# Half-width score products, a written TensorE order and a ScalarE copy in a gated-linear-attention stage

## The chip, the cores and the metric

The kernel runs on one core of a Trainium2 chip. The metric is the device time of one execution in microseconds (us), the median over several runs. A core has TensorE (matrix products; PE in the profile, with PEld for its weight loads), VectorE (DVE), ScalarE (ACT), GpSimd (POOL) and SyncE (SP), which issues most of the DMA transfers. Operands lie in SBUF tiles; TensorE's results go to PSUM, which this kernel uses as eight banks of 128 partitions by 512 float32 values. Each engine has its own list of instructions, and semaphores order one engine's behind another's.

## What is computed

The reference is a two-layer decoder trunk over 512 tokens of width 1024, in float32. Layer 0 mixes by windowed attention and a short convolution, layer 1 by gated linear attention (GLA); each layer has a gated feed-forward block with a convolution and a gated embedding. The change lies wholly in GLA, which has 4 heads with keys of 128 and values of 256:

```
log_a = log_sigmoid(g_lr @ w_gate_up + gate_bias) / 16
def step(state, inp):                    # one chunk of tokens, one head
    g = cumsum(log_a)
    o_inter = (q * exp(g)) @ state
    scores[t, s] = sum_d q[t, d] * k[s, d] * exp(g[t, d] - g[s, d])   for s <= t
    o_intra = scores @ v
    state = exp(g_end) * state + (k * exp(g_end - g)).T @ v
o = rms_norm(o_inter + o_intra) * silu(og);  y = o @ w_out
```

## The kernel before, in words

Activations lie feature by token: a tile holds 128 features by 512 tokens. A projection is `mm3` (L153): both operands are split into a high and a low part, and three products (L157 to L159) add up in one PSUM bank. Weights come through `weights`, `raw` and `cut` (L109 to L151): SyncE loads up to 1 MB into one of two `raw` buffers, ScalarE writes the high parts (`wh`, L137) and VectorE the low parts (`wl`, L138), with three buffers each. PSUM is used as four banks `ps` for projections and four banks `pa` for everything else.

`mixer1` (L1075) is the GLA stage. `query`, `key` and `gate` (L1121 to L1135) are projections of 24 products of 128x512 each, `Values` (L1086) makes the values in two steps of 48 products. For the scores the tokens are taken in NT = 4 blocks of 128. Within a block the pairs s < t are covered by levels b = 64, 32, ..., 1: level b holds the pairs in which s lies in the first and t in the second half of the same 2b tokens. For each head h:

- `base` (L1201): the running sum G of the log decays (VectorE, L1204), then the product of keys and queries of the even tokens (L1211), summed over features on TensorE with a matrix of ones (L1213) and written by VectorE to the diagonal of `sc` (L1215), which GpSimd has zeroed (L1214).
- `decay` (L1221), levels 64 to 4: a tile F whose first halves are k exp(G_mid - G) and whose second halves are q exp(G - G_mid); VectorE and ScalarE take turns.
- `level` (L1238): products of F with itself. For b < 64 one product per block, with all 128 columns of the block as weights and the 64 columns of the second halves moving (L1246); VectorE copies only the wanted entries to `sc` under a mask (L1253). For b = 64 a product of 64 weight columns by 64 (L1249), copied by L1255.
- `decay_pairs` and `level_pairs` (L1257, L1274): levels 2 and 1 share one product of 128x128 per block (L1280). For it VectorE scales every other key in place, and GpSimd copies the scaled queries into every other query (L1272). Two masked copies follow (L1284, L1289).
- `decay_off`, `off` (L1295, L1319): factors to and from the block borders, three transposes on TensorE (L1324) and a copy by ScalarE (L1326).
- `state` (L1329): three products (L1337). Products 0 and 1 go to the two halves of one `pa` bank, product 2 to another; ScalarE copies product 0 out (L1344), VectorE adds the other two to the state (L1339).
- `read` (L1349): for each block j the scores times the values (L1360), plus the state's part for j > 0 (L1362). Blocks 0 and 1 share a bank, and so do 2 and 3. ScalarE sums the squares of each (L1364, an activation and a read of its accumulator), the root goes through GpSimd (L167), and VectorE scales (L1369).
- `turn` and `gated` (L1371, L1137): eight transposes (L1376) which ScalarE copies out (L1380), then the product with silu(og) (L1142) and its split.

The calls stand in a list at the end of `mixer1`. Tile, the layer that records the kernel, chooses each engine's order from priorities and its own estimates, so that instructions may leave the order of the list; it places the semaphore waits, and it lets an access to a PSUM bank wait for the access to the same bank that was recorded before it. Inside `tc.manual_schedule(engines={...})` the engines named keep the recorded order; `setup`, the attention stage and the last stage use that already.

A float32 product that isn't a transpose runs as two passes, each with its own weight load, so its count in the profile is twice that of the code.

Of the kernel before, what the change touches and what calls it, by code (L numbers as in the profile page):

```python
# [18 lines left out]
P = 128  # L19
S = 512  # L20
# [36 lines left out]
class Kernel:  # L57
# [1017 lines left out]
    def mixer1(self):  # L1075
# [4 lines left out]
        with tc.tile_pool(name="m1", bufs=1) as mp:  # L1080
# [31 lines left out]
            def pair_w(c0):  # L1112
                return self.weights(w_in[:, :, c0 : c0 + 256], ND, 256)
# [82 lines left out]

            first = lambda x, b: x.rearrange("p (n b) -> p n b", b=2 * b)[:, :, :b]
            second = lambda x, b: x.rearrange("p (n b) -> p n b", b=2 * b)[:, :, b:]
            scores, Gs, Fs = {}, {}, {}

            def base(h):  # L1201

                G = Gs[h] = mp.tile([P, S], F32, tag="G", name=self.nm("G"), bufs=2)
                nc.vector.tensor_tensor_scan(  # L1204
                    G, run.rearrange("p a b -> p (a b)"), las[h], 0.0, op0=ALU.mult, op1=ALU.add
                )
                sc = scores[h] = mp.tile([P, GDV * NT], F32, tag="sc", name=self.nm("sc"), bufs=3)

                pr = new()[:, : S // 2]
                ev = lambda x: x.rearrange("p (n b) -> p n b", b=2)[:, :, 0]  # L1210
                nc.vector.tensor_tensor(pr, ev(kT[h]), ev(qT[h]), ALU.mult)  # L1211
                pd = self.pa()[:, : S // 2]
# [25 lines left out]
            def level(h, levels):  # L1238
                A = scores[h][:, :S]
                for l in levels:  # L1240
                    b, F = LEVELS[l], Fs[h, l]
                    pl = self.pa()
                    for t in range(NT):
                        c = slice(t * P, (t + 1) * P)
                        if b < 64:
                            mm(second(pl[:, c], b), F[:, c], second(F[:, c], b), start=True, stop=True)  # L1246
                        else:
                            mid = t * P + b
                            mm(pl[:b, mid : mid + b], F[:, t * P : mid], F[:, mid : mid + b], start=True, stop=True)  # L1249
                    if b < 64:  # L1250
                        mk = second(msk[:, l, :], b).unsqueeze(1).to_broadcast([P, NT, 64 // b, b])
                        tv = lambda x: x.rearrange("p (t n b) -> p t n b", t=NT, b=2 * b)[:, :, :, b:]
                        nc.vector.copy_predicated(tv(A), mk, tv(pl))  # L1253
                    else:
                        nc.vector.tensor_copy(second(A[:b], b), second(pl[:b], b))  # L1255

            def decay_pairs(h):  # L1257


                G, k, q = Gs[h].rearrange("p (n b) -> p n b", b=4), kT[h], qT[h].rearrange("p (n b) -> p n b", b=4)  # L1260
                G2 = Gs[h].rearrange("p (n b) -> p n b", b=2)
                E = new()
                Ek, Eq = E[:, : S // 2], E[:, S // 2 :].rearrange("p (n b) -> p n b", b=2)
                nc.vector.tensor_tensor(Ek, G2[:, :, 1], G2[:, :, 0], ALU.subtract)
                nc.vector.tensor_tensor(
                    Eq, G[:, :, 2:], G[:, :, 1:2].to_broadcast([P, S // 4, 2]), ALU.subtract
                )
# [3 lines left out]
                nc.vector.tensor_tensor(Eq, Eq, q[:, :, 2:], ALU.mult)  # L1271
                nc.gpsimd.tensor_copy(q.rearrange("p n (u b) -> p n u b", b=2)[:, :, :, 0], Eq)  # L1272

            def level_pairs(h):  # L1274

                A = scores[h][:, :S]
                pl = self.pa()
                for t in range(NT):
                    c = slice(t * P, (t + 1) * P)
                    mm(pl[:, c], kT[h][:, c], qT[h][:, c], start=True, stop=True)  # L1280
                v4 = lambda x: x.rearrange("p (t n b) -> p t n b", t=NT, b=4)
                m4 = lambda l: msk[:, l, :].rearrange("p (n b) -> p n b", b=4)
                two, one = LEVELS.index(2), LEVELS.index(1)
                nc.vector.copy_predicated(  # L1284
                    v4(A)[:, :, :, 2:], m4(two)[:, :, 2:].unsqueeze(1).to_broadcast([P, NT, P // 4, 2]),
                    v4(pl).rearrange("p t n (u b) -> p t n u b", b=2)[:, :, :, :, 0],
                )
                v2 = lambda x: x.rearrange("p (t n b) -> p t n b", t=NT, b=2)[:, :, :, 1]
                nc.vector.copy_predicated(  # L1289
                    v2(A),  # L1290
                    msk[:, one, :].rearrange("p (n b) -> p n b", b=2)[:, :, 1].unsqueeze(1).to_broadcast([P, NT, P // 2]),
                    v2(pl),
                )

            def decay_off(h):  # L1295
                G, b = Gs[h], 64
# [22 lines left out]
            def off(h):  # L1319

                Es, Ec, tot = Fs[h, "off"]
                pt = self.pa()
                for i in range(NT - 1):
                    nc.tensor.transpose(pt[:, i * P : (i + 1) * P], Es[:, i * P : (i + 1) * P], self.ident)  # L1324
                kt = new()
                nc.scalar.copy(kt[:, : 3 * P], pt[:, : 3 * P])  # L1326
                Fs[h, "kt"] = kt
# [74 lines left out]
            key(w, 0)  # L1402
            key(w, 1)
            w = pair_w(256)
            base(0)
            decay(0, lo)
            query(w, 2)
            level(0, lo)
            decay(0, hi)
            decay_off(0)  # L1410
            decay_pairs(0)
            query(w, 3)
            w = pair_w(768)
            level(0, hi)
            level_pairs(0)
            off(0)
            base(1)
            decay(1, lo)
            key(w, 2)
            level(1, lo)  # L1420
            decay(1, hi)
            decay_off(1)
            decay_pairs(1)
            key(w, 3)
            v = Values(0, 336, 336)
            level(1, hi)
            level_pairs(1)
            off(1)
            v.step(0)
            base(2)  # L1430
            decay(2, lo)
            v.step(1)
            v = Values(336, 672, 336)
            state(0)
            level(2, lo)
            read(0)
            decay(2, hi)
            decay_off(2)
            decay_pairs(2)
            v.step(0)  # L1440
            level(2, hi)
            level_pairs(2)
            off(2)
            turn(0)
            base(3)
            decay(3, lo)
            v.step(1)
            w = pair_w(2064)
            state(1)
            level(3, lo)  # L1450
            read(1)
            decay(3, hi)
            decay_off(3)
            decay_pairs(3)
            gate(w, 0)
            level(3, hi)
            level_pairs(3)
            off(3)
            turn(1)
            state(2)  # L1460
            gate(w, 1)
            w = pair_w(2064 + 256)
            self.load_vectors_ffn(1)
            read(2)
            gate(w, 2)
            turn(2)
            state(3)
            gated(0)
            gated(1)
            gate(w, 3)  # L1470
            w = pair_w(2064 + 512)
            read(3)
            gated(2)
            gated(3)
            gate(w, 4)
            turn(3)
            gated(4)
            gate(w, 5)
            w = pair_w(2064 + 768)
            gated(5)  # L1480
            for m in (6, 7):
                gate(w, m)
                gated(m)
# [42 lines left out]
```

## Time and profile before

| | us |
|---|---|
| median of 3 runs | 1249.83 (1249.44 to 1250.25) |
| the profiled execution's own time | 1249.96 |
| its span in the trace | 1248.2 |
| PE busy | 1240.5 (99%) |
| PEld busy | 1031.6 (83%) |
| DVE busy | 799.0 (64%) |
| ACT busy | 562.3 (45%) |
| POOL busy | 56.0 (4%) |

The span is the stretch from the first to the last instruction of one profiled execution. Lines of the profile name the source line of the kernel before (L1246), the engine, the operation, the tile written and the tiles read, and the shape, and end with a count or a time; "idle before" is the time for which the engine did nothing just ahead of a group, with the instruction that ended it. A timeline row begins with its start and its length in us. Matrix products overlap in the pipe, so the distance of two starts is what one costs, and not its length.

### The profile page before, as it was taken

The numbers are of one execution on the slowest core, as the hardware profiler recorded it, in microseconds if no ns is written. First come the engines' busy times: TensorE is split into PE (matmuls) and PEld (weight loads), VectorE is DVE, ScalarE is ACT, GpSimd is POOL, SyncE is SP. The second block draws the span as 40 slices with busy tenths as digits, with TensorE's granted clock in tenths as the row PEclk, the third lists the DMA queues.
The fourth block names the chain that finished last, engine by engine and source line by source line (L and its number), as shares of the span: only waits on it lengthen the run. The fifth ranks groups of instructions, "written<-read, shape, count | busy, mean of one in ns | idle before, by whom it ended". The sixth has DMA issues, their size and how long they took to land.

```text
span 1248.2 us, 14882 instructions
## 1 busy us (share of the span) xinstructions
PE 1240.5 (99%) x5824; PEld 1031.6 (83%) x5824; DVE 799.0 (64%) x1227; ACT 562.3 (45%) x869; POOL 56.0 (4%) x156
## 2 busy tenths in 40 slices
PE   9999999999999999999999999999999999999998
PEld 8877788888888888888989988888888888888887
DVE  6886556777777633346679765557777777444495
ACT  7466344444444322234563554435444444233374
POOL 2500000000000000000100000000000000000000
PEclk9999999999999999999999999999999999999999
DMA  6322232223333222222322222232233333322411
GB/s 214 97 75 58 81 102 89 84 98 102 101 102 101 91 96 93 93 84 92 110 91 67 68 68 68 101 107 90 86 99 102 102 101 102 101 93 93 144 51 67
DMA packets 111002, 117.42 MB, mean 94 GB/s; under 512 B 2728, under 2 KB 106210, under 8 KB 110932
## 3 DMA queue, kind: packets, MB, share of 16 engines
q1 hardware_dynamic: 109568, 115.35, 28.6%
q0 software_dynamic: 560, 0.42, 0.3%
q8 instruction: 45, 0.74, 0.2%
q10 hardware_dynamic: 804, 0.70, 0.2%
q14 instruction: 25, 0.20, 0.1%
HBM read 114.37 MB, written 2.10 MB: 93 GB/s over the span
## 4 chain that ended last, share of the span: by engine, by line
PE 91%; DVE 4%; ACT 2%; issue 1%; POOL 1%; DVEq 0%; POOLq 0%; ACTq 0%
PE ps L157 27%; PE ps L158 27%; PE ps L159 27%; PE ps L947 1%; PE ps L945 1%; PE ps L946 1%; PE pa L1246 1%; DVE wl L138 1%; PE pa L1360 1%; PE pa L158 0%; PE pa L1337 0%; PE pa L595 0%; PE pa L192 0%; POOL rq L167 0%; PE pa L159 0%
## 5 line engine op out<-in xcount | busy, mean ns | idle before, releaser
L137 ACT ACTIVATE wh<-raw 128x1024 fp32r<-128x1024 f32 (+4 forms) x212 | 214.8, 1015 | 343.6 <-PE ps L158 302.8
L138 DVE TENSOR_TENSOR wl<-raw,wh 128x1024 fp32r<-128x1024 f32 (+4 forms) x212 | 246.7, 1164 | 156.7 <-ACT wh L137 155.7
L157 PE MATMUL ps<-a,wh 128*128 128x512 f32 x864 | 337.0, 390 | 0.0
L158 PE MATMUL ps<-a,wh 128*128 128x512 f32 x864 | 336.6, 390 | 0.0
L159 PE MATMUL ps<-a,wl 128*128 128x512 f32 x864 | 336.3, 389 | 0.0
L157 PEld LDWEIGHTS ps<-a,wh 128*128 128x128 f32 x864 | 162.2, 188 | 34.0 <-issue 0.7
L159 PEld LDWEIGHTS ps<-a,wl 128*128 128x128 f32 x864 | 162.2, 188 | 33.9
L158 PEld LDWEIGHTS ps<-a,wh 128*128 128x128 f32 x864 | 162.3, 188 | 33.6 <-issue 0.3
L788 DVE SCALAR_TENSOR_TENSOR zt<-z,vfa,zt 128x512 f32<-128x512 f32 x176 | 131.4, 749 | 3.7 <-ACT zt L786 0.6
L157 PE MATMUL ps<-b,wh 128*128 128x512 f32 x320 | 126.5, 396 | 0.5 <-ACT b L101 0.5
L159 PE MATMUL ps<-b,wl 128*128 128x512 f32 x320 | 125.3, 392 | 0.0
L158 PE MATMUL ps<-b,wh 128*128 128x512 f32 x320 | 124.9, 391 | 0.0
L785 DVE TENSOR_TENSOR z<-ps,R 128x512 f32<-128x512 f32 x88 | 60.4, 688 | 74.5 <-PE ps L159 74.5
L157 PE MATMUL ps<-four,wh 128*128 128x512 f32 x224 | 87.1, 389 | 0.0
L158 PE MATMUL ps<-four,wh 128*128 128x512 f32 x224 | 87.1, 389 | 0.0
L159 PE MATMUL ps<-four,wl 128*128 128x512 f32 x224 | 87.1, 389 | 0.0
L786 ACT ACTIVATE zt<-z,vfb 128x512 f32<-128x512 f32 x88 | 71.1, 810 | 5.2 <-DVE z L785 3.3
L157 PEld LDWEIGHTS ps<-b,wh 128*128 128x128 f32 x320 | 60.0, 188 | 13.8 <-ACT b L101 1.3
L159 PEld LDWEIGHTS ps<-b,wl 128*128 128x128 f32 x320 | 60.1, 188 | 12.5
L158 PEld LDWEIGHTS ps<-b,wh 128*128 128x128 f32 x320 | 60.1, 188 | 12.3
L810 ACT ACTIVATE zt<-zt 128x512 f32<-128x512 f32 x44 | 27.9, 633 | 74.8 <-DVE zt L788 74.8
L101 ACT ACTIVATE four<-zt 128x512 fp32r<-128x512 f32 x28 | 17.7, 633 | 77.3 <-DVE zt L813 77.3
(359 smaller groups left out, 1570.2 us busy)
## 6 DMA issues: line engine op xcount, KB each, us to landing
raw<-in_ffn_w_up_dram SPq DMA_DIRECT2D x44, 1024.0 KB, 5.1
raw<-in_ffn_w_down_dram SPq DMA_DIRECT2D x16, 1024.0 KB, 5.1
raw<-in_hy_w_in_dram SPq DMA_DIRECT2D x8, 1024.0 KB, 4.9
raw<-in_gla_w_in_dram SPq DMA_DIRECT2D x8, 1024.0 KB, 5.2
raw<-in_ffn_w_down_dram SPq DMA_DIRECT2D x8, 768.0 KB, 4.4
raw<-in_ple_w_gate_dram SPq DMA_DIRECT2D x6, 1024.0 KB, 5.0
raw<-in_gla_w_out_dram SPq DMA_DIRECT2D x4, 1024.0 KB, 5.0
raw<-in_gla_w_in_dram SPq DMA_DIRECT2D x4, 672.0 KB, 4.0
```

Of the source, the lines that this page charges most:

```text
L101: nc.scalar.activation(h, src, AF.Copy)
L137: nc.scalar.activation(hv, v, AF.Copy)
L138: nc.vector.tensor_tensor(lv, v, hv.bitcast(F32), ALU.subtract)
L157: mm(out, lh, rh, start=start, stop=False)
L158: mm(out, lh, rl, start=False, stop=False)
L159: mm(out, ll, rh, start=False, stop=stop)
L785: nc.vector.tensor_tensor(z[:, 2:], ps, R, ALU.mult)
L786: nc.scalar.activation(y, z[:, 2:], AF.Identity, scale=w2[:, f : f + 1], bias=bb[:, f : f + 1])
L788: nc.vector.scalar_tensor_tensor(out=y, in0=z[:, tap : tap + S], scalar=w[:, f : f + 1], in1=y, op0=ALU.mult, op1=ALU.add)
L810: nc.scalar.activation(y, y, AF.Gelu)
L945: mm(o, lh, rh, start=first and j == 0, stop=False, **kw)
L946: mm(o, lh, rl, start=False, stop=False, **kw)
```

## The change

The change has three parts, all in `mixer1`.

1. `level` for b < 64 and `level_pairs` make two products for each block: one for each half of its 64 tokens, with 64 weight columns, written to the matching half of the partitions. 64 moving columns become twice 32, and 128 become twice 64. Each masked copy becomes two of 64 partitions.
2. The list of calls stands inside `manual_schedule` for TensorE, in a new order. Projections and value steps stand between the parts of a head, and `base` gives its product of ones to a call of its own, `diagonal`.
3. The copy of the scaled queries moves from GpSimd to ScalarE.

```diff
-                            mm(second(pl[:, c], b), F[:, c], second(F[:, c], b), start=True, stop=True)
+                            for u in (0, 64):
+                                d = slice(t * P + u, t * P + u + 64)
+                                mm(second(pl[u : u + 64, d], b), F[:, d], second(F[:, d], b), start=True, stop=True)
...
-                        mk = second(msk[:, l, :], b).unsqueeze(1).to_broadcast([P, NT, 64 // b, b])
-                        tv = lambda x: x.rearrange("p (t n b) -> p t n b", t=NT, b=2 * b)[:, :, :, b:]
-                        nc.vector.copy_predicated(tv(A), mk, tv(pl))
+                        for u in (0, 64):
+                            r = slice(u, u + 64)
...
+                            mk = second(msk[r, l, r], b).unsqueeze(1).to_broadcast([64, NT, 32 // b, b])
+                            nc.vector.copy_predicated(tv(A), mk, tv(pl))
...
-                nc.gpsimd.tensor_copy(q.rearrange("p n (u b) -> p n u b", b=2)[:, :, :, 0], Eq)
+                nc.scalar.copy(q.rearrange("p n (u b) -> p n u b", b=2)[:, :, :, 0], Eq)
...
-                    mm(pl[:, c], kT[h][:, c], qT[h][:, c], start=True, stop=True)
+                for d0 in range(0, S, 64):
+                    d, u = slice(d0, d0 + 64), d0 % P
+                    mm(pl[u : u + 64, d], kT[h][:, d], qT[h][:, d], start=True, stop=True)
```

The list of calls after (a call of before is the same without `diagonal`; there `state(0)` stood between two value steps and `level(2, lo)`, and `turn(1)`, `state(2)`, `read(2)`, `turn(2)`, `state(3)` and `read(3)` behind the last `level_pairs` with gates between them):

```
with tc.manual_schedule(engines={ET.PE}):
    base(0); decay(0, lo); query(w, 2); diagonal(0); query(w, 3); w = pair_w(768)
    level(0, lo); decay(0, hi); decay_off(0); decay_pairs(0); key(w, 2); key(w, 3); v = Values(0, 336, 336)
    level(0, hi); level_pairs(0); off(0); base(1); decay(1, lo); v.step(0); diagonal(1)
    level(1, lo); decay(1, hi); decay_off(1); decay_pairs(1); v.step(1); v = Values(336, 672, 336); v.step(0); state(0)
    level(1, hi); level_pairs(1); off(1); base(2); read(0); decay(2, lo); v.step(1); w = pair_w(2064); diagonal(2)
    level(2, lo); turn(0); decay(2, hi); decay_off(2); decay_pairs(2); gate(w, 0); state(1); gate(w, 1); w = pair_w(2064 + 256)
    level(2, hi); level_pairs(2); off(2); base(3); read(1); decay(3, lo); gate(w, 2); diagonal(3)
    level(3, lo); turn(1); decay(3, hi); decay_off(3); decay_pairs(3); state(2); gate(w, 3); w = pair_w(2064 + 512); self.load_vectors_ffn(1)
    level(3, hi); level_pairs(3); off(3); read(2); gate(w, 4); gated(0); gated(1); turn(2); state(3); gate(w, 5); w = pair_w(2064 + 768)
    read(3); gated(2); gated(3); gate(w, 6); gated(4); gated(5); turn(3); gate(w, 7); gated(6); gated(7)
```

More of the change, by code (lines that the diff above doesn't have):

```diff
@@ L1198, in mixer1 @@
             second = lambda x, b: x.rearrange("p (n b) -> p n b", b=2 * b)[:, :, b:]
+            ev = lambda x: x.rearrange("p (n b) -> p n b", b=2)[:, :, 0]
             scores, Gs, Fs = {}, {}, {}
@@ L1207, in base, with diagonal @@
                 sc = scores[h] = mp.tile([P, GDV * NT], F32, tag="sc", name=self.nm("sc"), bufs=3)
-                pr = new()[:, : S // 2]
-                ev = lambda x: x.rearrange("p (n b) -> p n b", b=2)[:, :, 0]
+                pr = Fs[h, "pr"] = new()[:, : S // 2]
                 nc.vector.tensor_tensor(pr, ev(kT[h]), ev(qT[h]), ALU.mult)
+            def diagonal(h):
+                sc, pr = scores[h], Fs[h, "pr"]
                 pd = self.pa()[:, : S // 2]
@@ L1404, in mixer1 @@
             w = pair_w(256)
[L1405 to L1483, printed above, removed]
+            with tc.manual_schedule(engines={ET.PE}):
+                base(0)
+                decay(0, lo)
+                query(w, 2)
+                diagonal(0)
+                query(w, 3)
+                w = pair_w(768)
+                level(0, lo)
+                decay(0, hi)
+                decay_off(0)
+                decay_pairs(0)
+                key(w, 2)
+                key(w, 3)
+                v = Values(0, 336, 336)
+                level(0, hi)
+                level_pairs(0)
+                off(0)
+                base(1)
+                decay(1, lo)
+                v.step(0)
+                diagonal(1)
+                level(1, lo)
+                decay(1, hi)
+                decay_off(1)
+                decay_pairs(1)
+                v.step(1)
+                v = Values(336, 672, 336)
+                v.step(0)
+                state(0)
+                level(1, hi)
+                level_pairs(1)
+                off(1)
+                base(2)
+                read(0)
+                decay(2, lo)
+                v.step(1)
+                w = pair_w(2064)
+                diagonal(2)
+                level(2, lo)
+                turn(0)
+                decay(2, hi)
+                decay_off(2)
+                decay_pairs(2)
+                gate(w, 0)
+                state(1)
+                gate(w, 1)
+                w = pair_w(2064 + 256)
+                level(2, hi)
+                level_pairs(2)
+                off(2)
+                base(3)
+                read(1)
+                decay(3, lo)
+                gate(w, 2)
+                diagonal(3)
+                level(3, lo)
+                turn(1)
+                decay(3, hi)
+                decay_off(3)
+                decay_pairs(3)
+                state(2)
+                gate(w, 3)
+                w = pair_w(2064 + 512)
+                self.load_vectors_ffn(1)
+                level(3, hi)
+                level_pairs(3)
+                off(3)
+                read(2)
+                gate(w, 4)
+                gated(0)
+                gated(1)
+                turn(2)
+                state(3)
+                gate(w, 5)
+                w = pair_w(2064 + 768)
+                read(3)
+                gated(2)
+                gated(3)
+                gate(w, 6)
+                gated(4)
+                gated(5)
+                turn(3)
+                gate(w, 7)
+                gated(6)
+                gated(7)
```

29 lines of the change are left out of this document (15 added, 14 removed).

## The prediction

> **What bounds the kernel now.** I read the page first, then TensorE's groups by form, then timelines in the linear-attention (GLA) stage, which runs from about 600 to 790 us.
>
> ```profile
> span 1248.2 us, 14882 instructions
> PE 1240.5 (99%) x5824; PEld 1031.6 (83%) x5824; DVE 799.0 (64%) x1227; ACT 562.3 (45%) x869; POOL 56.0 (4%) x156
> ...
> PEclk9999999999999999999999999999999999999999
> ```
>
> TensorE is busy for 99% of the span, at full clock, so time changes only as its work shrinks, or as it is made to wait. VectorE is loaded, but late nowhere for long:
>
> ```profile
> 642.20:668.00 25.80, 25.71 (x149) 21.45 (x149) 25.80 (x67) 11.67 (x21) 2.35 (x1) 1.00 0.18 54
> ```
>
> Here VectorE has no idle time, and TensorE still lacks only 0.1 of 25.8 us.
>
> The groups of TensorE's weight loads show where it waits, and for whom (last column: idle time before the group, and its releaser):
>
> ```profile
> L1246 PEld LDWEIGHTS pa<-F 128*128 128x128 f32 x128 | 15.8, 191 | 0.7
> L1249 PEld LDWEIGHTS pa<-F 128*64 128x64 f32 x32 | 2.2, 137 | 1.4 <-PE ps L158 0.4 <-DVE mx L1300 0.4 <-PE pa L1337 0.3
> L1280 PEld LDWEIGHTS pa<-qT,kT 128*128 128x128 f32 x32 | 3.9, 191 | 0.7 <-POOL qT L1272 0.7
> L1337 PEld LDWEIGHTS pa<-vt,F 128*128 128x128 f32 x24 | 4.1, 189 | 1.0 <-ACT st L1344 0.4
> L1360 PEld LDWEIGHTS pa<-vt,sc 128*128 128x128 f32 x32 | 5.3, 189 | 1.9 <-ACT osq L1364 1.4
> ```
>
> Before the change the waits for other engines here are 1.4 + 0.4 + 0.7 = **2.5 us**, on ScalarE's reads of `state` and `read` and on GpSimd's strided copy. Each written product counts twice, since a float32 product runs as two passes: 64 level products are x128.
>
> **Part 1: two halves instead of one product.** A timeline of `level(0, lo)`:
>
> ```profile
> 648.22 0.39 PE L158 MATMUL ps<-b,wh 128*128 128x512 f32 x1
> 648.45 0.39 PE L159 MATMUL ps<-b,wl 128*128 128x512 f32 x1
> 648.76 0.54 PEld L1249 LDWEIGHTS pa<-F 128*64 128x64 f32 x8 [0.35 <-DVE mx L1300]
> 649.37 2.75 PEld L1246 LDWEIGHTS pa<-F 128*128 128x128 f32 x24
> ```
>
> 24 loads of 128 columns take 2.75 us, one of them 0.191: (2.75 - 0.19)/23 = 0.111 us apart. Eight loads of 64 columns: (0.54 - 0.137)/7 = 0.058 apart. Half the columns load in half the time, so the weight load sets these products. The change turns 160 passes (128 + 32) into 320 of 64 columns, whose outputs go to the two halves of the partitions in turn. All hangs on whether the two halves run at the same time. The attention stage has such a pair (L658, `po[64 * g : 64 * g + 64]`):
>
> ```profile
> 105.17 0.20 PEld L658 LDWEIGHTS pa<-pT,v 128*64 128x64 f32 x4 [0.35 <-issue]
> 105.17 1.94 PE L658 MATMUL pa<-pT,v 128*64 128x512 f32 x8
> 761.06 0.59 PE L1362 MATMUL pa<-st,F 128*128 128x256 f32 x2
> L1362 PE MATMUL pa<-st,F 128*128 128x256 f32 x24 | 7.1, 379 | 0.0
> ```
>
> Two passes with 256 moving columns start 0.59 - 0.379 = 0.21 us apart, so passes with 512 stand 0.43 apart, and of eight in a row the last would start after 7 x 0.43 = 3.0 us. All eight are done in 1.94: two at a time, the last pair starting after 3 x 0.43 = 1.3. Even four weight loads stand within 0.20. So I take a pair of halves at 0.058 us for the 0.111 of one product: 160 x (0.058 - 0.111) = **-8.5 us**. If they run one after another it is 160 x (0.116 - 0.111) = +0.8, and both ends are kept.
>
> Going to 64-column weights and back costs TensorE something: L1249 begins 0.31 after the last L159, where 0.23 is usual (648.22 to 648.45), and its eight take 0.61 to the next group instead of 8 x 0.058 = 0.46; with that 0.15, about 0.25 for a visit. Before, each head makes one visit, after it two (`level(h, hi)` with `level_pairs(h)` is the second): 4 x 0.25 = **+1.0 us**.
>
> **Part 2: the written order.** In the built program of the change TensorE holds exactly the order of the calls. The blocks of decays, projections and values stand far apart: `level(0, lo)` follows two whole projections (48 products of 0.23, 11 us) after `base(0)`. So I expect no wait for the decays. What the written order also fixes is the inside of `state` and `read`. `state` makes products 0 and 1 in the two halves of one bank, and ScalarE copies 0 out (L1344) before 1 is emitted; `read` does the same twice, with the square sums (L1364). In the built program, before and after, the second product of a bank waits for ScalarE's read of the first. Before, the recorded order puts other work in between; after it, the second product stands directly behind the first four times in `state` and eight times in `read`, and everything else of TensorE is queued behind it. What such a wait lasts:
>
> ```profile
> 759.08 1.02 PE L1360 MATMUL pa<-vt,sc 128*128 128x256 f32 x4
> 760.02 0.36 ACT L1364 ACTIVATE osq<-pa 128x256 f32<-128x256 f32 x1
> 760.28 0.19 ACT L1364 ACTIVATION_READ_ACCUMULATOR osq<-pa 128x1 f32 x1
> 760.52 0.30 PEld L1360 LDWEIGHTS pa<-vt,sc 128*128 128x128 f32 x2 [0.39 <-ACT osq L1364]
> 763.18 0.59 PE L1362 MATMUL pa<-st,F 128*128 128x256 f32 x2
> 763.87 0.39 ACT L1364 ACTIVATE osq<-pa 128x256 f32<-128x256 f32 x1 [0.76 <-PE pa L1362]
> 764.15 0.20 ACT L1364 ACTIVATION_READ_ACCUMULATOR osq<-pa 128x1 f32 x1
> 736.09 1.03 PE L1337 MATMUL pa<-vt,F 128*128 128x256 f32 x4
> 736.72 0.37 ACT L1344 COPY st<-pa 128x256 f32<-128x256 f32 x1 [0.30 <-PE pa L1337]
> 737.18 0.42 PEld L1337 LDWEIGHTS pa<-vt,F 128*128 128x128 f32 x2
> ```
>
> The weight load at 760.52 stands 0.05 after ScalarE's second instruction ends at 760.47. With ScalarE free: products end at 763.77, ScalarE reads from 763.87 to 764.35, the next product could start at 764.40; without the wait it starts at 763.18 + 0.43 = 763.61. That is **0.79 us** for each of eight in `read`. In `state`: 737.18 instead of 736.09 + 0.43 = 736.52, **0.67 us** for each of four. The least sum is 8 x 0.79 + 4 x 0.67 = 9.0 us.
>
> ScalarE isn't always free. I walked its built order with these durations (0.1 off from each to the next, as the instructions at 760.02 and 760.28 overlap; a transpose of L1376 lasts 0.272 and follows after 0.109):
>
> ```profile
> 751.18 1.03 PE L1376 MATMUL pa<-cf,sc 128*128 128x128 f32 x8
> L1380 ACT ACTIVATE oT<-pa,vec 128x512 f32<-128x512 f32 x8 | 5.2, 680 | 0.0
> L1135 ACT ACTIVATE og<-og 128x512 f32<-128x512 f32 x6 | 3.8, 625 | 0.0
> L1310 ACT ACTIVATE F<-F 128x384 f32<-128x384 f32 x4 | 2.1, 525 | 0.4 <-DVE F L1304 0.3
> L1326 ACT COPY F<-pa 128x384 f32<-128x384 f32 x4 | 1.9, 481 | 5.7 <-PE pa L1324 5.7
> L1234 ACT ACTIVATE F<-G 128x256 f32<-128x256 f32 x4 | 1.7, 420 | 1.9 <-DVE G L1204 1.9
> L1313 ACT ACTIVATE F<-F 128x192 f32<-128x192 f32 x4 | 1.4, 362 | 0.7 <-DVE F L1312 0.7
> L1314 ACT ACTIVATE mx<-mx 128x4 f32<-128x4 f32 x4 | 0.8, 199 | 0.9 <-DVE F L1304 0.9
> L1135 ACT ACT_TABLE_LOAD x1 | 1.3, 1283 | 0.0
> ```
>
> - `state(2)` follows `turn(1)`. Between its first product and its copy ScalarE does two copies of `turn` (0.68 each), a table load (1.28), exponentials of 0.53, 0.36, 0.36 and 0.20, then the copy (0.37): 4.46 in all. It starts 3 x 0.109 + 0.27 + 0.1 = 0.7 after the transposes begin and ends at 0.7 + 4.46 - 0.7 = 4.5; TensorE was ready at 8 x 0.109 + 0.43 = 1.3. Wait 3.2.
> - `state(3)` follows `turn(2)`: two copies and a silu (0.62) ahead of the copy: 0.7 + 2.35 - 0.3 = 2.8, wait 1.5. `state(0)` and `state(1)`: 0.9 and 0.7.
> - The first wait of `read(1)`: ahead of the square stand `off`'s copy (0.48), a table load and an exponential (0.42): `off`'s transposes end after 0.6, 0.6 + 2.76 - 0.4 = 3.0, and TensorE was ready at 3 x 0.109 + 0.43 = 0.76: 2.2. In the same way `read(2)`, behind a table load, a silu and a copy that begin earlier: 1.5; `read(0)`, behind a copy and an exponential: 1.0; `read(3)`, behind nothing: 0.8.
> - The second waits of `read`: 0.8, 1.0, 0.8, 0.9, where 0.8 has nothing ahead.
>
> Sum: 6.3 + 5.5 + 3.5 = **+15.3 us**. The 2.5 us of waits before go: they are these same waits and the GpSimd one. That **-2.5** is the only place where the old order's gaps are credited.
>
> ScalarE's table loads rise from two to six in the stage, since silu (`gate`) and exponentials (`decay`) now alternate there. They cost only through the waits above.
>
> **Part 3: copies.**
>
> ```profile
> L1253 DVE COPY_PREDICATED sc<-msk,pa 128x256 f32<-128x256 uint8 x16 | 7.0, 434 | 4.6 <-PE pa L1246 4.4
> L1284 DVE COPY_PREDICATED sc<-msk,pa 128x256 f32<-128x256 uint8 x4 | 2.9, 729 | 0.0
> L1272 POOL COPY qT<-F 128x256 f32<-128x256 f32 x4 | 3.6, 900 | 62.9 <-DVE F L1271 45.8 <-ACT wh L137 17.1
> ```
>
> 24 predicated copies become 48 of half the partitions and half the elements. Each lies between half its time and all of it, so VectorE gains nothing and pays at most 16 x 0.43 + 8 x 0.73 = 12.8 us over four heads. `scores` is read a head's length later, which hides most; where VectorE is full, what is behind it (the diagonal of the next head, which holds one of the four banks that `level` needs) comes late. I take **+0.7** for that, between 0 and 3 (a quarter of 12.8). The strided copy moves from GpSimd (0.90) to ScalarE (0.42 as L1234, same size); its wait is in the 2.5. No DMA moves: SyncE's order is the same.
>
> **Sum**: -8.5 + 1.0 + 15.3 - 2.5 + 0.7 = **+6.0 us** on the profiled execution's 1249.96 us (span 1248.2), which is 0.13 above the median of 1249.83: **1256.0 us**.
>
> **Rivals.**
> - *A, the halves don't gain.* The pair needs four instructions in 0.058 us, and the fastest long run here is L1249: sixteen in 8 x 0.058 = 0.46, 0.029 each. If that is what TensorE can be fed, a pair takes 0.116 and the -8.5 is +0.8: 1265.3. For it: no row shows more than sixteen short instructions at a higher rate. Against it: L658's loads, four in 0.20 where one lasts 0.137 as in L1249. [...]
> - *B, the other side: ScalarE is never late.* The twelve waits are at their least, 9.0: -8.5 + 1.0 + 9.0 - 2.5 + 0.7 = -0.3, 1249.7. If the halves besides load as in L658, 0.02 apart, so that a pair takes about 0.04, it is 160 x (0.04 - 0.111) = -11.4, and 1246.8. It decides once the waits sum to less than 8.5 - 1.0 + 2.5 - 0.7 = 9.3: 0.78 each, hardly more than their least. Against it: the built order of ScalarE has the table loads and copies in front.
> - *C, VectorE becomes the bound.* Copies cost what whole ones did: +3 instead of +0.7, 1258.3. For it: the stretch with no idle VectorE.
>
> **How the numbers follow.** Forecast 0.57 (own range 1252.5 to 1260, with C in its upper part). A 0.20 (fed in part 1260, not at all 1265). B 0.18: 0.10 near 1249.7, 0.08 faster. Something else slower, 0.05. Without B's faster part, half of B's other part and the tail from A's own value on, 0.8 is left: 1249.5 to 1265.5. About 0.2% (2.5 us) is what a measurement of this kernel can tell from no change: faster 0.08, same 0.12, slower 0.80.
>
> **What would show it.** L1246's successor: the pair period in its timeline, 0.06 or 0.11 us (part 1, A). The weight loads of `state` and `read`: idle time 15 us, released by ScalarE's st and osq, in place of 1.8 (part 2; near 9 is B). Their longest single one in `state(2)`, with a table load on ScalarE in it. TensorE busy about 8 us less, the stage longer. The prediction is wrong if those idle times are absent, or if TensorE waits for VectorE's decays instead.

## The result, and the profile after

The kernel after takes **1262.14 us** (median of 5 runs, 1261.1 to 1263.66) against 1249.83 (1249.44 to 1250.25): a ratio of 1.010, interval 1.0089 to 1.0111, or 12.3 us slower. The profiled execution has a span of 1260.1 us and a time of its own of 1261.87.

Lines have moved: the level products of before (L1246) are L1252, the pair products (L1280) L1290, `state` with its copy (L1337, L1344) is L1347 and L1354, `read` with its square sums (L1360, L1364) is L1370 and L1374. The page of after, its head and its row of the granted clock:

```profile
span 1260.1 us, 15229 instructions
...
PE 1237.7 (98%) x5984; PEld 1025.3 (81%) x5984; DVE 804.2 (64%) x1251; ACT 567.3 (45%) x877; POOL 52.8 (4%) x152
...
PEclk9999999999999999999999989999999999999999
```

TensorE is busy for 2.8 us less and the span is 11.9 us longer, so TensorE waits. One slice of the clock row is an 8: for 6.83 us of the trace's clock records TensorE was granted 0.50 and not its full clock, which no slice of before shows. TensorE's weight loads by group (busy time, mean ns of one, then the idle time before and who ended it):

```profile
L1252 PEld LDWEIGHTS pa<-F 128*64 128x64 f32 x256 | 8.6, 137 | 2.4 <-issue 1.4 <-ACT F L1234 0.6 <-PE pa L1347 0.3
L1290 PEld LDWEIGHTS pa<-qT,kT 128*64 128x64 f32 x64 | 2.2, 138 | 0.0
L1347 PEld LDWEIGHTS pa<-vt,F 128*128 128x128 f32 x24 | 4.5, 212 | 8.3 <-ACT st L1354 7.7 <-issue 0.2
L1370 PEld LDWEIGHTS pa<-vt,sc 128*128 128x128 f32 x32 | 5.2, 188 | 11.6 <-ACT osq L1374 11.2
```

The idle time released by `st` and `osq` is 7.7 + 11.2 = 18.9 us; before it was 0.4 + 1.4. The wait of the GpSimd copy is gone (L1290 has none).

Of the 12.3 us, 12.1 lie in the GLA stage: from its first decay product to the norm behind it, 204.7 us became 216.8. I added up, line by line, the distance from the start of one product of TensorE to the start of the next, so that the sums make up the stage:

| products of the stage | before | after | difference |
|---|---|---|---|
| level and pair products, with their visits and waits | 19.6 | 11.9 | -7.7 |
| `state` | 5.3 | 13.0 | +7.7 |
| `read`, scores times values | 7.4 | 16.9 | +9.6 |
| projections and values | 155.7 | 158.1 | +2.5 |
| the rest | 16.9 | 16.9 | 0.0 |

**The halves** do what part 1 says. The weight loads of `level(0, lo)` in a timeline:

```profile
653.79 0.54 PEld L1255 LDWEIGHTS pa<-F 128*64 128x64 f32 x8 [0.35 <-DVE F L1322]
654.19 1.54 PEld L1252 LDWEIGHTS pa<-F 128*64 128x64 f32 x48
```

48 loads in 1.54 us, one of them 0.137: (1.54 - 0.137)/47 = 0.030 apart, 0.060 for a pair, where one whole product took 0.111.

**The longest wait** is that of `state(2)`, in the timeline of ScalarE and TensorE:

```profile
744.46 1.27 ACT L1390 ACTIVATE oT<-pa,vec 128x512 f32<-128x512 f32 x2 [0.27 <-PE pa L1386]
744.96 0.67 PE L1347 MATMUL pa<-vt,F 128*128 128x256 f32 x2
745.74 1.28 ACT L1320 ACT_TABLE_LOAD   x1
747.04 0.52 ACT L1320 ACTIVATE F<-F 128x384 f32<-128x384 f32 x1
747.47 0.35 ACT L1321 ACTIVATE F<-G 128x192 f32<-128x192 f32 x1
747.72 0.35 ACT L1323 ACTIVATE F<-F 128x192 f32<-128x192 f32 x1
747.97 0.19 ACT L1324 ACTIVATE mx<-mx 128x4 f32<-128x4 f32 x1
748.07 0.35 ACT L1354 COPY st<-pa 128x256 f32<-128x256 f32 x1
748.47 1.35 PEld L1347 LDWEIGHTS pa<-vt,F 128*128 128x128 f32 x4 [3.25 <-ACT st L1354]
```

Two copies, a table load and four exponentials stand ahead of the copy that TensorE waits for. Its second product loads 0.05 us after that copy ends.

**The clock** falls just then. The table of stretches (each row: the stretch, its length, busy time of PE, PEld, DVE, ACT and POOL with their instructions, the granted clock, DMA) with stretches of 3.41 us:

```profile
744.04:747.45 3.41, 1.57 (x10) 0.86 (x8) 3.25 (x9) 3.12 (x5) 0.00 (x0) 1.00 0.00 0
747.45:750.87 3.42, 2.40 (x6) 1.95 (x7) 3.15 (x8) 2.13 (x7) 0.00 (x0) 0.50 0.73 240
750.87:754.28 3.41, 3.41 (x10) 2.67 (x9) 1.01 (x3) 0.43 (x1) 0.00 (x0) 0.50 0.19 66
754.28:757.70 3.42, 3.42 (x17) 2.74 (x16) 0.00 (x0) 0.05 (x1) 0.00 (x0) 1.00 0.00 0
```

and the weight loads of the projection behind `state(2)`, where the clock comes back:

```profile
752.90 0.33 PEld L158 LDWEIGHTS ps<-b,wh 128*128 128x128 f32 x1
753.33 0.33 PEld L159 LDWEIGHTS ps<-b,wl 128*128 128x128 f32 x1
753.76 0.33 PEld L157 LDWEIGHTS ps<-b,wh 128*128 128x128 f32 x1
754.18 0.24 PEld L158 LDWEIGHTS ps<-b,wh 128*128 128x128 f32 x1
754.47 0.19 PEld L159 LDWEIGHTS ps<-b,wl 128*128 128x128 f32 x1
754.70 0.19 PEld L157 LDWEIGHTS ps<-b,wh 128*128 128x128 f32 x1
```

For 6.83 us the clock is 0.50, and products that stand 0.23 apart stand 0.43 apart. The stretch ahead of it, with TensorE busy for 1.57 of 3.41 us, was still granted the full clock.

### The profile page after: what moved, and what is told of

Read it like the earlier page. It is cut to its first block, busy times and chain, and to the rows that moved or that the text cites. A ratio compares the mean times of both kernels' runs of the same rounds, so it can differ in the third digit from the quotient of the medians.

```text
span 1260.1 us, 15229 instructions
## 1 busy us (share of the span) xinstructions
PE 1237.7 (98%) x5984; PEld 1025.3 (81%) x5984; DVE 804.2 (64%) x1251; ACT 567.3 (45%) x877; POOL 52.8 (4%) x152
## 4 chain that ended last, share of the span: by engine, by line
PE 91%; DVE 4%; ACT 3%; issue 1%; POOL 1%; DVEq 0%; ACTq 0%; POOLq 0%
PE ps L157 27%; PE ps L158 27%; PE ps L159 27%; PE ps L947 1%; PE ps L946 1%; PE ps L945 1%; DVE wl L138 1%; ACT wh L137 1%; PE pa L595 0%; PE pa L1347 0%; PE pa L158 0%; PE pa L1252 0%; PE pa L192 0%; PE pa L1370 0%; PE pa L159 0%
## 5 line engine op out<-in xcount | busy, mean ns | idle before, releaser
L158 PEld LDWEIGHTS ps<-b,wh 128*128 128x128 f32 x320 | 60.6, 189 | 12.7
```

What stands on the lines that cost most here:

```text
L158: mm(out, lh, rl, start=False, stop=False)
```

## The experiments

My theory after the result: the twelve waits of a product for ScalarE's read of the other half of its bank cost some 18 us, the half clock that follows the longest of them 2.5 to 3, and the halves give some 7 back. Rivals: the waits only show work that ScalarE has late anyway, so they would come back elsewhere; or the halves themselves bring the waits or the clock.

### Are the waits the cost?

`both_first` changes nothing in the order of TensorE. It only emits both products of a bank before either is read, so that none has a read ahead of it:

```diff
-                    if i:
-                        nc.vector.scalar_tensor_tensor(
...
-                    else:
-                        nc.scalar.copy(st[:, i, :], u)
+                    us.append(u)
+                nc.scalar.copy(st[:, 0, :], us[0])
+                for i in range(1, NT - 1):
+                    nc.vector.scalar_tensor_tensor(
...
-                    nc.scalar.activation(sq, po, AF.Square, accum_out=oss[:, j : j + 1])
+                    if j % 2:
+                        for i in (j - 1, j):
...
+                            nc.scalar.activation(sq, pos[i], AF.Square, accum_out=oss[:, i : i + 1])
```

> The kernel after with one thing changed: in state and read both products of a bank are emitted before ScalarE (or VectorE) reads either, so no product waits for a read of its own bank. Main theory: the idle time of the weight loads behind osq and st falls from 18.9 us to below 1, the restart costs of 0.1 each go, and with the long wait in state(2) the half-clock stretch goes: 1262.1 - 16.0 - 1.2 - 2.7 = 1242 us. Rival D (ScalarE is late anyway, so that the next user of its results, turn or the next bank, waits instead): 1250 to 1258 us.

Measured: 1243.25 us (1242.72 to 1243.56), ratio to before 0.9949 (0.9936 to 0.9961). 18.9 us of after are gone, and the version is 6.4 us faster than before. Its weight loads and its clock:

```profile
L1252 PEld LDWEIGHTS pa<-F 128*64 128x64 f32 x256 | 8.6, 137 | 2.6 <-ACT F L1234 1.5 <-issue 0.7 <-PE pa L1348 0.3
L1371 PEld LDWEIGHTS pa<-vt,sc 128*128 128x128 f32 x32 | 5.8, 190 | 1.0 <-issue 0.3
L1348 PEld LDWEIGHTS pa<-vt,F 128*128 128x128 f32 x24 | 4.4, 189 | 0.7 <-PE pa L1389 0.2
```

```profile
PEclk9999999999999999999999999999999999999999
```

The waits for `st` and `osq` are gone and the clock stays full. The rival falls: little came back elsewhere (`turn` and `off` start 1.1 us later in sum).

`state_both_first` and `read_both_first` do this in one of the two alone.

> The kernel after with both products of a bank emitted before either is read in state alone; read keeps its waits. The rows of after charge 7.7 us more to the start of state's products than in the version without waits. Theory (waits add up one by one, and the clock depends on which windows of 3.41 us they leave thin): 1262.1 - 7.7 = 1254.4 us if read(1)'s wait falls into one window and takes the clock down, 1252 us if not. Rival (a wait removed in state comes back in read or turn): 1258 us or more.

> The kernel after with both products of a bank emitted before either is read in read alone; state keeps its four waits. Theory: read's products start 10.0 us earlier in sum than in after; the wait of 3 us in state(2) stays and may take the clock down: 1262.1 - 10.0 = 1252.1 us, or 1249.7 if the window is not thin enough. Rival (waits removed in read come back elsewhere): 1256 us or more.

Measured: 1254.05 us (1252.1 to 1254.47) and 1252.43 (1250.81 to 1253.62), ratios to before 1.0031 (1.0018 to 1.0043) and 1.0022 (1.0012 to 1.0032). Against after that is 8.1 and 9.7 us, 17.8 together, and 18.9 when both are done. The waits add up, as the theory wants. Most of the width of the runs goes with the clock: in `state_both_first` two runs with a mean clock of 1.0 took 1252.1 and 1252.46 us, two with 0.997 took 1254.43 and 1254.47 (but one with 0.999 took 1254.42); in `read_both_first` the run with 1.0 took 1250.81 us, those with 0.999 and 0.998 took 1251.63 to 1252.64, and those with 0.997 took 1252.8 to 1253.62. The profiled run of `state_both_first` has its half clock behind the wait of `read(1)`, at 731 us, since that of `state(2)` isn't there.

### What makes the waits long?

`no_silu` takes table loads from ScalarE. It leaves out the nonlinearity of the gates:

```diff
-nc.scalar.activation(g, g, AF.Silu)
+nc.scalar.activation(g, g, AF.Copy)
```

> The kernel after with the gates' silu replaced by a plain copy of the same tile (the gates' nonlinearity is left out), which needs no table, so that ScalarE's table loads in the stage fall from six to two or fewer; its exponentials, copies and squares stay, in whatever order they then get. Theory (table loads of 1.28 us in front of ScalarE's reads are what makes the long waits long): the waits of state(2), read(1) and read(2) fall by 2.1, 1.2 and 0.8 us to near 1, and no window of 3.41 us is thin enough to take the clock down: 1262.1 - 4.1 - 2.7 = 1255.3 us. Rival (the order of ScalarE's other work makes the waits, loads hardly matter): 1260 us or more.

Measured: 1254.37 us (1254.02 to 1255.13), ratio to before 1.004 (1.0025 to 1.0055). The stage has 3 table loads of 1.28 us instead of 8 (two of them stand ahead of the written order in both kernels), and the weight loads

```profile
L1370 PEld LDWEIGHTS pa<-vt,sc 128*128 128x128 f32 x32 | 5.2, 189 | 10.1 <-ACT osq L1374 9.8
L1347 PEld LDWEIGHTS pa<-vt,F 128*128 128x128 f32 x24 | 4.0, 189 | 5.9 <-ACT st L1354 5.3 <-PE pa L1386 0.2
```

wait 3.8 us less (18.9 to 15.1). By distances of starts the wait of `state(2)` and the first ones of `read(1)` and `read(2)`, which the theory names, fall to 0.6, 1.0 and 0.7 us. The longest idle time of the weight loads is now 1.9 us for both, in place of 2.6 and 3.2: that of `state(3)`, as in after, and that of the second wait of `read(1)`, which grew. No stretch of the stage is at half clock. In this kernel's ScalarE order the copy of `state(2)` also stands ahead of some of the exponentials, so that not all of the 3.8 us is loads. The theory's 1255.3 holds: table loads lengthen the longest waits, and with them gone the clock stays. But most of the waiting, 15.1 us, is there without them.

### Are the halves worth what was forecast?

`halves_alone` is the kernel before with the new `level` and `level_pairs` and nothing else. `order_whole` is the kernel after with the old ones.

> The kernel before with part 1 alone (64-column products and halved masked copies; no written order, copy still on GpSimd). Main theory: the halves gain 8.5 us, 4 more visits to 64 columns cost 1.2, VectorE's copies about 0.7, and no wait for ScalarE comes: 1249.8 - 6.6 = 1243 us, full clock. Rival A (the halves don't gain, or their thin load lets the clock fall): 1250 us or later.

> The kernel after with part 1 undone (whole products and whole masked copies; written order and ScalarE copy kept). Main theory: the twelve waits in state and read are all there (about 19 us of idle weight loads released by osq and st), the half-clock stretch too, since it follows the wait in state(2), and the halves' 6.6 us are given back: 1262.1 + 6.6 = 1268.7 us. Rival (the halves bring the clock down or lengthen the waits): no half-clock stretch, 1266 us or less.

Measured: 1249.55 us for `halves_alone`, ratio 1.0001 (0.9991 to 1.001), and 1264.18 for `order_whole`, ratio 1.0117 (1.0103 to 1.0131). Both theories miss. Without the written order the halves bring nothing, and with it 2.0 us instead of 6.6. The rivals come nearer in time, but not for their reasons: the halves do shorten the products, `halves_alone` has the full clock, and `order_whole`, without any halves, has the waits (9.2 + 8.0 us of idle weight loads) and the half clock. So the halves cause neither the waits nor the half clock. TensorE's waits in `halves_alone`, between 600 and 800 us:

```profile
PE pa L1287 <- POOL qT L1279: 1.9, 2, 1.5
PE pa L1213 <- DVE F L1211: 0.5, 1, 0.5
PE ps L157 <- DVE kT L1129: 0.5, 1, 0.5
PE ps L158 <- DVE wl L138: 0.3, 1, 0.3
```

```profile
640.00:660.00 20.00, 18.45 (x155) 14.88 (x154) 19.75 (x49) 8.35 (x15) 1.28 (x1) 1.00 0.18 50
660.00:680.00 20.00, 18.62 (x155) 14.18 (x154) 18.96 (x51) 6.91 (x14) 0.91 (x1) 1.00 0.10 30
```

Its level products take 10.6 us instead of 15.0, and its pair products 2.5 instead of 4.2, both without their waits for GpSimd (2.3 and 0.4): 6.1 us shorter. All of it is lost again, in two ways. From 640 to 680 us VectorE is busy for 38.7 of 40 us, and TensorE, done sooner, now has 2.9 us without work, behind VectorE and behind GpSimd's copy, which waits for VectorE itself. This is rival C, in an order in which the levels of the first head stand close together. The other way is TensorE's order itself, which Tile chose anew and which isn't quite that of before: the 64-column products stand in 16 separate places of the stage, where before has 4 and after 8. Behind each place the first pass starts 0.12 us late and the second 0.06 to 0.11 (at 650.05 and 650.38 us two passes stand 0.33 apart that usually stand 0.23). Sixteen times some 0.2 us is, as an estimate from these starts, the other 3 us. The expectation had counted four more visits, not twelve.

In `order_whole` the products cost 18.5 us and in after 11.9, a gain of 6.7. But `state` and the scores times values of `read` together cost 27.2 us there and 30.0 in after: TensorE comes sooner to the same ScalarE work and waits longer for it (TensorE's longest wait in `read` is 1.1 us in `order_whole` and 2.2 in after). After also loses 0.7 us more in the projections and 0.7 in `off` and `turn`, which stand behind visits to 64-column weights there; the half clock of `order_whole` lasts one stretch of 3.41 us, that of after two.

`whole_both_first` has the written order, no same-bank waits, and whole products: the two edits above together.

> The kernel after with whole products and whole masked copies, and with both products of a bank emitted before either is read: the written order without the same-bank waits and without the halves. Theory 1 (in the written order VectorE is not in the way, so the halves are worth their 7.4 us of shorter products where nothing else waits): 1243.25 + 7 = 1250 us. Theory 2 (the halves gain only a third of that in any order, as from 1264.2 to 1262.1): 1245.5 us.

Measured: 1247.5 us (1246.78 to 1248.08), ratio 0.9983 (0.9973 to 0.9992), between the two theories: the halves bring 4.25 us here. Their products are 6.8 us shorter than the whole ones (19.0 to 12.1 with waits), and 1.8 us are lost at the transposes of `off` and `turn`, which now wait for VectorE, and 0.5 in `state` and `read`.

So the halves bring 0.0 us in the order that Tile chooses, 2.0 in the written order with its waits, and 4.25 in the written order without them, while the products themselves are 6 to 7 us shorter each time.

`halves_actcopy` is `halves_alone` with part 3's ScalarE copy.

> The kernel before with the 64-column halves and with the strided copy on ScalarE, still without the written order. The halves alone came out at 1249.55 us: their 6.5 us of shorter products went into new waits, 2.3 us of them behind GpSimd's strided copy, the rest behind VectorE. Theory 1 (the order recorded before leaves VectorE full from 642 to 680 us, so TensorE only waits where it was quicker; GpSimd's copy is one of several ends of that chain): the GpSimd wait turns into one for VectorE or ScalarE, 1248 to 1250 us. Theory 2 (GpSimd's 0.9-us copy itself is what eats the gain): 1249.6 - 2.3 or more, 1247 us or less.

Measured: 1248.67 us, ratio 0.9994 (0.9984 to 1.0003), 0.9 less than `halves_alone`. By starts the waits for the copy are 1.5 us shorter and the products of `base` start 0.9 later, and the 16 separate places are still there: theory 1.

`both_first_pool` asks the same of the written order: `both_first` with the copy on GpSimd.

> The version without same-bank waits (1243.25 us), with its strided copy back on GpSimd (0.90 us in place of 0.42). Theory: key and query stand ahead of level_pairs in the written order, so the copy is off the path: within 0.5 us of 1243.25. Rival (the copy is on the path, as in the order recorded before): a wait of TensorE for GpSimd of 0.5 us for each of four heads, 1245 us.

Measured: 1243.18 us (1242.46 to 1243.84), no difference. In the written order the copy's engine doesn't matter.

### The clock

Could the clock fall because of the thin halves, and not the wait? `fill` keeps the wait and gives TensorE something to do in it, into a bank that nobody reads:

```diff
 nc.scalar.copy(st[:, i, :], u)
+if h == 2:
+    self.nowhere = self.ps()
+    self.idle(12)
```

> The kernel after with twelve idle products of 512 columns (0.227 us each, 2.7 us in all, into a bank that nobody reads) put between the first and the second product of state(2), inside its wait of 2.9 to 3.2 us. Theory that the long wait brings the clock down: the second product starts at the same time as before, the clock stays full behind it, and the time is 1262.1 - 2.7 = 1259.4 us. Rival (the clock falls for another reason, such as the thin halves and transposes ahead of it): the half-clock stretch stays, 1262 us or, if the fillers are run at half clock and outlast the wait, up to 1264.5.

Measured: 1260.4 us (1260.19 to 1261.76). In the profiled run (1261.76) the clock stays full behind `state(2)`, as the theory has it, but there is a half clock elsewhere, behind the wait of `read(1)`:

```profile
728.63:732.04 3.41, 1.18 (x6) 1.01 (x6) 3.32 (x10) 3.15 (x7) 0.00 (x0) 0.99 0.01 2
732.04:735.45 3.41, 2.79 (x8) 1.70 (x7) 3.41 (x9) 2.21 (x6) 0.00 (x0) 0.50 0.01 2
```

That wait is 2.6 us here and in after. In after it is split between two stretches of the 3.41-us grid (2.10 and 1.99 us busy), here it falls into one, of which TensorE was busy for 1.18 us. The three other runs have a mean clock of 1.0 and take 1260.19 to 1260.61. So the same program loses its clock in some runs and in others not. `fill_two` puts nine idle products into the wait of `read(1)` as well.

> The kernel after with idle products put inside its two longest waits: nine (2.0 us) in the first wait of read(1) and twelve (2.7 us) in that of state(2). With twelve in state(2) alone the half-clock stretch moved to the wait in read(1), where a window of 3.41 us of the clock records was busy for only 0.35. Theory (the clock is set for windows of 3.41 us on a fixed grid, by how busy TensorE was in the one before, and falls somewhere below 0.55): no window is left under 0.5, the clock stays at 1.0, and the time is 1262.1 - 2.7 = 1259.4 us with a range of its runs no wider than that of the kernel before (0.8 us). Rival (the clock falls for another reason): a half-clock stretch again, 1260.5 to 1262.5 us.

Measured: 1259.67 us (1258.65 to 1260.05), ratio 1.008 (1.0065 to 1.0096); the clock is full throughout the profiled run and 0.999 or 1.0 in all. The time is the theory's, but the runs spread over 1.4 us where at most 0.8 was expected. The thinnest stretch of the profiled run, around the first wait of `read(2)`:

```profile
755.84:759.25 3.41, 1.78 (x10) 1.23 (x9) 3.32 (x6) 2.72 (x7) 0.00 (x0) 1.00 0.00 0
```

With the twelve waits kept and the clock back, the time is 2.5 us less than after's by the medians, and the stage of the profiled runs is 2.8 us shorter (216.8 and 214.1). That is what the clock costs, and the wait is what brings it down.

### A better order?

`turn_earlier` changes `both_first` by one call:

```diff
+                turn(1)
                 diagonal(3)
                 level(3, lo)
-                turn(1)
```

> The version without same-bank waits (1243.25 us) with turn(1) moved ahead of diagonal(3) and level(3, lo) in the written order. There TensorE still waits 1.1 us, in level(3, lo), for VectorE's diagonal, which frees a bank. Theory (turn's eight transposes, 0.9 us, fill that wait): 1242.3 us. Rival (turn is early for VectorE then, whose scaled copies it needs, and takes two of the four banks itself): 1243.3 to 1244 us.

Measured: 1246.91 us (1245.76 to 1247.87), 3.7 more than `both_first`. Neither theory gave that. One wait became longer and took the clock with it, and two waits for ScalarE are new:

```profile
PE pa L1252 <- DVE sc L1218: 1.5, 1, 1.5
PE pa L1371 <- ACT vfb L217: 1.0, 1, 1.0
PE pa L1290 <- ACT qT L1282: 0.5, 1, 0.5
```

```profile
735.97:739.38 3.41, 1.91 (x54) 1.75 (x52) 3.35 (x9) 3.38 (x4) 0.00 (x0) 1.00 0.00 0
739.38:742.80 3.42, 3.42 (x13) 2.73 (x10) 3.29 (x9) 2.28 (x7) 0.00 (x0) 0.50 0.00 0
```

VectorE's diagonal comes later still, and the stretch with that wait also holds thin transposes and halves. By distances of starts the stage is 3.9 us longer than that of `both_first`: 0.8 is the longer wait, 1.5 the half clock (in `state(2)` and the projection behind it), and 1.9 are the two new waits, in `level_pairs(3)` and ahead of `read(2)`. `both_first` stays the best version of the study, at 1243.2 us.

## Why the prediction was wrong, point by point

The direction, the waits and their places were right; the sum was +6.0 where +12.3 was measured. **The step that failed is part 2's sum of +15.3**, which held the waits alone, and with it the credit for before: together, the 2.5 without GpSimd's 0.7, they make +15.3 - 1.8 = +13.5 for `state`, `read` and what follows from their waits, and the stage shows 7.7 + 9.6 + 2.5 = +19.8. The 1262.1 us lie beyond the forecast's own range (1252.5 to 1260); that the wide range holds them is luck, since it reaches so far for rival A, which had no part in it.

- *Part 1, -8.5 + 1.0.* Right for the products: a pair takes 0.060 us, taken as 0.058. With the visits, their share of part 3 and GpSimd's wait, the prediction makes it -8.5 + 1.0 + 0.7 - 0.7 = -7.5; the stage shows -7.7, with 1.1 us behind the visits charged to other rows (0.4 to the projections, 0.7 to `off` and `turn`). As a statement on the time it would have been wrong: alone the halves bring nothing.
- *Part 2, the walk of ScalarE's order.* Nearly right. By distances of starts, less the usual 0.216 us, the waits are, in the prediction's order (forecast in brackets): `state` 1.1 (0.9), 0.9 (0.7), 3.0 (3.2), 1.7 (1.5); first waits of `read` 0.9 (1.0), 2.4 (2.2), 1.8 (1.5), 1.0 (0.8); second waits 0.8 (0.8), 0.9 (1.0), 0.8 (0.8), 0.8 (0.9). Sum 16.1 in place of 15.3.
- *What part 2 left out.* First, the pass behind one that waited starts 0.32 us after it instead of 0.22; twelve times 0.1 is 1.2 us. It can be read in before's trace as well (760.52 to 760.84 us). Second, the clock: 2.1 us in the projections (158.1 us in after, 156.0 in `fill_two`) and 0.7 in the end of `state(2)`, where passes stand 0.43 to 0.59 apart. The prediction showed a full clock in before and didn't ask what a wait of 3.2 us would do to it.
- *The credit of -2.5.* Too large. It took idle time of the weight loads as time. By starts, `state` and `read` of before cost 12.7 us and without any wait (`whole_both_first`) 11.6, so that 1.1 of the 1.8 us were real: in the rest of that idle time the trace has earlier products running.
- In sum: walk 0.8, late second passes 1.2, clock 2.1 + 0.7, projections behind visits 0.4, credit 0.7: 5.9 of the 6.3 us that were missing.
- *TensorE busy about 8 us less.* This sign didn't come: it is 2.8 us less, since the half clock (2.8 us) and the late second passes (1.2 us) count as busy time, by an estimate from the sums above.
- *Part 3.* Right in size. Masked copies are 295 and 440 ns long where whole ones were 434 and 729:

```profile
L1263 DVE COPY_PREDICATED sc<-msk,pa 64x128 f32<-64x128 uint8 x32 | 9.4, 295 | 1.1 <-PE pa L1252 0.3
L1296 DVE COPY_PREDICATED sc<-msk,pa 64x128 f32<-64x128 uint8 x8 | 3.5, 443 | 0.2
L1282 ACT COPY qT<-F 128x256 f32<-128x256 f32 x4 | 1.7, 430 | 3.1 <-DVE F L1281 3.1
```

  VectorE is at them 3.7 us longer over the stage (16 x (2 x 0.295 - 0.434) + 8 x (2 x 0.44 - 0.73)), and the waits of TensorE for VectorE and ScalarE in front of level products are 1.1 us (forecast 0.7).
- *Rival A* falls: 320 short passes are fed at 0.027 to 0.030 us each (16 loads in 0.55 us, 48 in 1.54). *Rival B* falls: the waits sum to 16.1 us where their least is 9.0. *Rival C* isn't what happened in after, but in `halves_alone` it takes about half of the gain.

What stays open: how thin a stretch must be for the clock to fall. In the traces, stretches with 0.55 (`read_both_first`), 1.18 (`fill`), 1.19 (`state_both_first`), 1.45 (`order_whole`) and 1.57 us (after) of 3.41 busy lost it, and those with 1.70 (`fill`, near its end), 1.78 (`fill_two`) and 1.87 (after) kept it, which, as an estimate from these times, puts a limit between 0.46 and 0.50 of a stretch. But the stretch of `turn_earlier` with 1.91 (0.56) lost it as well. It is filled with short passes, 54 of them; whether these count for less wasn't tried.

## What to carry to other kernels

When an order is written down by hand, emit all products of a bank before the first read of it: the wait between two products is set by the place of that read on its engine, and here it was worth 18.9 us of a stage of 217, the clock included. Price a shorter product by what TensorE meets sooner behind it: the same 6 to 7 us of shorter products were worth 0, 2.0 or 4.25 us, as VectorE or ScalarE were late, and as often as TensorE had to go to 64-column weights and back. Price an added wait at its length, at 0.1 us more for the pass behind it (0.32 us in place of 0.22 here), and at the clock where it leaves a stretch of 3.41 us as empty as that of `state(2)`: TensorE was busy for 1.57 us of it, and the half clock behind it cost 2.8 us.

## What the runs showed of the hardware

- In these traces the granted clock changed in steps of 3.41 us: in their clock records the half clock of after lasts 6.83 us, that of `order_whole` and `turn_earlier` 3.41, and after's full clock before it 740.69 us, which is 217.0 steps. It fell behind a step in which TensorE was busy for 0.55 to 1.57 us (and for 1.91 in `turn_earlier`), so where the grid lies counts: the 2.6-us wait of `read(1)` took the clock down in `fill`, where it fell into one step, and not in after, where two steps shared it. The gaps between products ahead of it were 2.8 us long in after, 2.2 in `fill` and 1.5 in `turn_earlier`.
- Two products with 64 weight columns each, written to the two halves of the partitions, took 0.055 to 0.060 us a pair in the 320 passes of after (16 loads in 0.55 us, 48 in 1.54), as long as one pass of before's L1249, whose products all go to one half (0.058). A masked copy with half the partitions and half the elements on each took 0.6 to 0.7 of the time of the whole one (295 ns for 434, 440 for 729).
